# A recurrent layer and an attention layer on one core: first norm rows by products with ones, a fourth place for loaded weights, another order at several seams

## The chip, the cores and the metric

The kernel runs as one program on 1 core of a Trainium2 chip. The metric is the device time of one execution in microseconds (us); of several runs the median counts. The engines are TensorE (PE in the profile, its weight loads are PEld), VectorE (DVE), ScalarE (ACT), GpSimd (POOL) and SyncE (SP), which before the change issues every transfer.

## The reference, cut to what matters

```python
def rms_norm(x, g):
    return x * rsqrt(mean(x * x, axis=-1) + 1e-6) * g

def lru_mixer(h, ...):                       # layer 0, width 1536 in 12 blocks of 128
    u = h @ w_in                             # 1024 x 1024 times 1024 x 3072
    xb, gate = u[..., :1536], u[..., 1536:]
    xc = causal_depthwise_conv(xb, conv_w, conv_b)      # 4 taps
    r = sigmoid(block_diag(xc, wa) + ba); i = sigmoid(block_diag(xc, wx) + bx)
    log_a = -8 * r * softplus(-a_param)
    bterm = sqrt(-expm1(2 * log_a)) * (i * xc)
    hs = scan(exp(log_a), bterm)             # first-order recurrence over the sequence
    return (hs * silu(gate)) @ w_out

def fox_mixer(h, w_in, b_f, w_out):          # layer 1, 16 heads of 64
    q, k, v, gate, f_logit = split(h @ w_in) # 4 * 1024 + 16 columns
    cum = cumsum(log_sigmoid(f_logit + b_f)) # one row for each head
    logits = q @ k.T / 8 + cum[q] - cum[k]   # causal
    return (softmax(logits) @ v * silu(gate)) @ w_out

x = x + lru_mixer(rms_norm(x, norm_g[0]))
x = x + fox_mixer(rms_norm(x, norm_g[1]))
out = rms_norm(x, final_g)                   # 1024 x 1024, float32
```

## The kernel before, in words

The sequence (1024) is worked on in two halves of 512; activations lie with the features on the 128 partitions. Nearly every product is a float32 one made of three passes: each operand is split into a high part and a rest (`wh`/`wl` for weights, `hh`/`hl` for activations), and the passes are high by high, high by rest and rest by high. ScalarE makes the high part (`to_hi`, lines 80 to 92), VectorE or GpSimd the rest (`to_lo`, L96). A weight block goes through three tiles: `wf` (as loaded; 3 places), `wh` and `wl` (4 places each).

The order of instructions on each engine is set ahead of time by the language's scheduler, which follows the order of the code, generators that the code advances by hand (`run`, `take`, `drain`) and `issue_after` marks, which put an instruction behind a named one in that order. Every engine then runs its own list in order and waits on semaphores.

The program has these stages.

1. **First norm** (0 to about 58 us). The first layer's input product doesn't wait for the norm: it runs on `x * g`, and the row of inverse roots, `rs`, is multiplied in when a result is taken out of PSUM (`us`, L271, and `gps`). `inv_rms` (L136 on) makes `rs` for one half: eight products 128x1 with a column of ones sum the squares into `sscol`; ScalarE takes roots of the 128x4 result, VectorE the reciprocals (L147) and four diagonal matrices (L149); one product of ones with them spreads the row over all partitions (`rsrow`, L151), and ScalarE copies it to `rs` (L152). For n = 2 the product `ups` needs the PSUM banks that `us` of n = 0 has to empty first.
2. **Recurrent layer** (to about 430 us): a loop over 12 blocks with `ups` and `gps` products, gates, `recur` (tanh, exp, square, root, scan) and output products `ops`.
3. **Second norm, values, forget gates** (to about 510 us). `values(g)` makes V for four heads: eight sequence tiles `st`, each 8 by 3 products into one PSUM tile `vps`, which ScalarE and VectorE empty. Call 0 also makes the 16 forget logits (`fz`); `forget` transposes them (`fps`, L58), and accumulates them into `cum`, which goes through DRAM into operands `T` and `U` of the score product.
4. **Attention** (to about 1098 us): for 16 heads, `maxima` makes scores `S`, adds the mask and takes maxima `m` (L678), and exponentials `p` with row sums (L683); `weigh` transposes `p` (`pt`), splits it and multiplies by V (`O`). Beside them PE is filled with the next pair's key, query and gate products, with `values(1)` to `values(3)` after heads 3, 7 and 11, and late with output products `ops`. The inverse row sums go to DRAM and come back spread over 64 partitions (`recd`, L697, and `recb`, L701); GpSimd multiplies them into the gate (`sg`, L710) and the gate into the head's output (`yo`, L765). `split_y` splits `yo` for the last pairs (`yhh`, `yhl`). `partial` adds `ops` to `xp` and stores it to DRAM (`x1d`, L842).
5. **Turning and the last norm** (to the end). `turned` adds the last two pairs' product to the transposed residual in `turn`; ScalarE squares and sums (`sq`, L891), VectorE multiplies by the final weights, `root_mean` (L909 to L912) gives the factor, and L897/L898 scale.

Of the kernel before, what the change touches and what calls it, by code (L numbers as in the profile page):

```python
# [38 lines left out]
def trunk(ctx: ExitStack, tc: tile.TileContext, xt, w0, wg, wo0, pc, gn, gf, w1, wv, wf, bf, wo1, out):  # L39
# [57 lines left out]

    def split_weights(src, shape, hi_eng, lo_eng, parts=wpool):
        wt = wpool.tile([P, *shape], F32, tag="wf", name="wf", bufs=3)
# [75 lines left out]
    with ExitStack() as l0:  # L175
# [3 lines left out]
        tmp = lru.enter_context(pool("t0", 1, side="right"))  # L179

# [77 lines left out]

        for _ in zip(split_x(0), square_x(0)):
            pass  # L260
# [7 lines left out]
        def conv(n, ups):  # L268
# [10 lines left out]
            wt = wpool.tile([P, 4, P], F32, tag="wf", name="wgf", bufs=3)[:, :2]  # L279
# [30 lines left out]
        def recur(n, parts=(slice(0, SEQ),)):  # L310
# [4 lines left out]
            for cs in parts:  # L315
# [10 lines left out]
                nc.scalar.activation(t_, t_, AF.Sqrt, scale=1.0 / 16.0)  # L326
# [15 lines left out]
        def out_weights(g, d0):  # L342

            wt = wpool.tile([P, 4, P], F32, tag="wf", name="wf", bufs=3)
# [25 lines left out]
        for n in range(NB):  # L370
# [8 lines left out]
            if n == 0:  # L379
# [4 lines left out]
                done = rms_row(sums[0], rs[:, :HALF])[1]  # L384
# [34 lines left out]
        outputs(NB - 1, halves, silu(state[NB - 1], gps, halves))  # L419
        lru.close()  # L420
# [50 lines left out]
    with ExitStack() as l1:  # L471
# [4 lines left out]
        mask = tu.tile([P, SEQ], BF16, name="mask")  # L476
        nc.gpsimd.memset(mask, 0.0)
        nc.gpsimd.affine_select(
            out=mask, in_=mask, pattern=[[-1, SEQ]], compare_op=ALU.is_ge, fill=NEG, base=SEQ - P, channel_multiplier=1
        )  # L480


# [5 lines left out]
        for s in range(2):  # L488
            nc.gpsimd.memset(f32(T[s][64:, 1]), 1.0)
            for u in U[s][s:]:  # L490
                nc.vector.memset(f32(u[64:, 1]), 0.0)
                nc.vector.memset(f32(u[64:68, 1]), -1.0)
# [9 lines left out]
        def values(g):  # L502
# [11 lines left out]
            for st in range(8):  # L514
                if ex and st % 2:
                    pt = ps.tile([P, SEQ], F32, tag="S", name="vps")[:, : 256 + ex]
                else:
                    pt = ps.tile([P, 256 + ex], F32, tag="g", name="vps")
                c = (st % 4) * P
                for k in range(KT):  # L520
                    xh, xl = hT[st // 4][k]
                    wh, wl = parts[k]
                    xh, xl = xh[:, c : c + P], xl[:, c : c + P]
# [3 lines left out]
                    if k % 4 == 1:  # L527
                        yield
# [542 lines left out]
```

## Time and profile before

| | |
|---|---|
| three runs | 1137.04, 1137.51, 1138.75 us; median 1137.51 us |
| the profiled execution | 1138.24 us; its span, from first to last instruction, 1136.5 us |
| granted clock of TensorE | 0.999 |
| busy: VectorE, ScalarE, GpSimd | 757.9 us (67%), 592.1 us (52%), 163.5 us (14%) |
| transfers | 105.43 MB, all but the instruction queues on one hardware queue; its packets took 31.8% of the 16 engines' span |
| the chain that ended last, in its last stretches | `turn` products 18.55 us from 1112.07 us, then squares, root, reciprocal, scaling and the output's transfers to 1136.5 us |

A row of the trace's timeline reads: start, duration, engine, line, operation, result<-operands, shape, and in brackets how long the engine had been idle before it and what it had waited for. Matmuls are pipelined, so the duration of one is longer than the distance to the next; the distance between two starts is what a product costs. A row of the waits reads: total us, how many times, the longest.

### The profile page before, as it was taken

Reading aid. Unit: us, or ns where it says so; the run is one execution under the profiler, and the core shown is the slowest. Engines: PE = TensorE matmul, PEld = TensorE weight load, DVE = VectorE, ACT = ScalarE, POOL = GpSimd, SP = SyncE. Lnnn points to the kernel's source line nnn. Section 1 sums busy time; section 2 is a strip of 40 time slices with the busy share of each in tenths; the row PEclk is TensorE's granted clock in tenths of the full one; section 3 lists DMA queues with packets and bytes.
Section 4 is the critical chain, followed back from the end, with each engine's and each line's share of the span. In section 5 each row is a group of like instructions: output and inputs, shape, how many; then the busy total and the mean of one; then the engine's idle time right before and its main releaser. Section 6 shows DMA issues by size and latency. Waiting matters only on the chain.

```text
span 1136.5 us, 15822 instructions
## 1 busy us (share of the span) xinstructions
PE 1116.5 (98%) x5713; PEld 937.5 (82%) x5713; DVE 757.9 (67%) x1276; ACT 592.1 (52%) x1081; POOL 163.5 (14%) x105
## 2 busy tenths in 40 slices
PE   8999999999999999999999999999999999999997
PEld 7787888888888887888888888888888888878886
DVE  7589756876568689666676466764666645676645
ACT  8388345354453666365555355553555534554435
POOL 1212112121121201420010100101001010010110
PEclk9999999999999999999999999999999999999999
DMA  6111121111202114433525215242142431665445
GB/s 215 52 42 51 42 61 38 52 51 42 61 28 61 51 53 147 130 108 95 121 71 117 71 59 123 80 108 79 58 116 78 114 86 47 180 176 164 155 145 185
DMA packets 63702, 105.43 MB, mean 93 GB/s; under 512 B 9508, under 2 KB 24484, under 8 KB 63624
## 3 DMA queue, kind: packets, MB, share of 16 engines
q1 hardware_dynamic: 63624, 104.42, 31.8%
q8 instruction: 45, 0.74, 0.3%
q14 instruction: 33, 0.27, 0.1%
HBM read 63.30 MB, written 15.93 MB: 70 GB/s over the span
## 4 chain that ended last, share of the span: by engine, by line
PE 89%; DVE 3%; ACT 2%; issue 2%; DMA 2%; POOL 1%; SPq 0%; POOLq 0%; ACTq 0%; DVEq 0%
PE gps L54 33%; PE ops L54 15%; PE ups L54 11%; PE vps L54 7%; PE S L54 6%; PE O L54 6%; PE pt L58 5%; PE turn L54 3%; PE gate L54 2%; DVE sq L162 1%; POOL wl L96 1%; DMA x<-in_xt 1%; DVE wl L96 0%; DVE x L453 0%; DMA wf<-in_wo 0%
## 5 line engine op out<-in xcount | busy, mean ns | idle before, releaser
L54 PE MATMUL gps<-hh,wh 128*128 128x512 f32 x576 | 228.9, 398 | 0.0
L54 PE MATMUL gps<-hl,wh 128*128 128x512 f32 x576 | 226.7, 394 | 0.0
L54 PE MATMUL gps<-hh,wl 128*128 128x512 f32 x576 | 226.6, 393 | 0.0
L85 ACT CAST wh<-wf 128x512 fp32r<-128x512 f32 (+2 forms) x156 | 94.3, 607 | 144.2 <-PE gps L54 47.2
L683 ACT ACTIVATE p<-S,m 128x128 f32<-128x128 f32 (+7 forms) x128 | 94.9, 741 | 135.5 <-DVE m L678 134.4
L96 POOL TENSOR_TENSOR wl<-wf,wh 128x512 fp32r<-128x512 f32 (+1 forms) x60 | 98.1, 1639 | 395.9 <-ACT wh L85 342.8
L96 DVE TENSOR_TENSOR pl<-pt,ph 128x512 fp32r<-128x512 f32 (+1 forms) x198 | 98.6, 540 | 81.3 <-ACT ph L85 81.0
L54 PEld LDWEIGHTS gps<-hl,wh 128*128 128x128 f32 x576 | 108.2, 188 | 24.5
L54 PEld LDWEIGHTS gps<-hh,wl 128*128 128x128 f32 x576 | 108.6, 189 | 19.8
L54 PEld LDWEIGHTS gps<-hh,wh 128*128 128x128 f32 x576 | 108.5, 188 | 19.8
L678 DVE CUSTOM_DVE_ANT_0 S<-S,mask 128x128 f32<-128x128 f32 (+7 forms) x128 | 97.3, 760 | 30.5 <-PE S L54 28.9
L710 POOL TENSOR_TENSOR sg<-sg,recb 64x1024 f32<-64x1024 f32 (+1 forms) x17 | 39.2, 2306 | 460.2 <-DMA recb<-recd 444.6
L85 ACT CAST ph<-pt 128x512 fp32r<-128x512 f32 (+1 forms) x198 | 83.6, 473 | 30.6 <-PE pt L58 25.3
L54 PE MATMUL S<-T,U 96*128 96x512 f32 (+7 forms) x384 | 92.2, 349 | 2.0 <-ACT p L683 2.0
L96 DVE TENSOR_TENSOR wl<-wf,wh 128x512 fp32r<-128x512 f32 x96 | 72.1, 756 | 26.0 <-ACT wh L85 25.3
L361 DVE TENSOR_TENSOR x<-x,ops 128x512 f32<-128x512 f32 x80 | 54.0, 681 | 50.6 <-PE ops L54 50.6
L54 PEld LDWEIGHTS S<-T,U 128*128 128x128 f32 (+1 forms) x384 | 68.7, 190 | 15.9 <-ACT p L683 3.2
L54 PE MATMUL ups<-hh,wh 128*128 128x512 f32 x192 | 75.9, 395 | 4.3 <-ACT hh L87 2.4
L58 PE MATMUL pt<-ident,p 128*128 128x128 f32 x576 | 79.3, 273 | 0.0
L58 PEld LDWEIGHTS pt<-ident,p 128*128 128x128 f32 x576 | 67.4, 140 | 12.4 <-issue 2.2
L54 PE MATMUL vps<-wh,hh 128*128 128x256 f32 (+1 forms) x256 | 73.7, 288 | 3.0 <-DVE sg L649 2.1
L54 PE MATMUL ops<-yh,wh 128*128 128x512 f32 x192 | 76.1, 396 | 0.5 <-DVE x L453 0.5
(176 smaller groups left out, 2259.0 us busy)
## 6 DMA issues: line engine op xcount, KB each, us to landing
wf<-in_w SPq DMA_DIRECT2D x100, 256.0 KB
wf<-in_wo SPq DMA_DIRECT2D x64, 128.0 KB
U<-qkh SPq DMA_DIRECT2D x64, 128.0 KB
T<-qkh SPq DMA_DIRECT2D x28, 256.0 KB
x<-in_xt SPq DMA_DIRECT2D x16, 256.0 KB
x1d<-x SPq DMA_DIRECT2D x16, 256.0 KB
wf<-in_wv SPq DMA_DIRECT2D x16, 256.0 KB
U<-qkl SPq DMA_DIRECT2D x32, 128.0 KB
```

What stands on the lines that cost most here:

```text
L54: pe[0] = nc.tensor.matmul(*args, **kw)
L58: pe[0] = nc.tensor.transpose(*args)
L85: nc.scalar.copy(hi, src)
L96: return eng.tensor_tensor(lo, src, f32(hi), ALU.subtract)
L162: eng.tensor_tensor(parts[0], parts[0], sq, ALU.add)
L361: nc.vector.tensor_tensor(x, x, pt, ALU.add)
L678: nc.vector.tensor_tensor_reduce(S[:, :n], S[:, :n], mask[:, SEQ - n :], -1.0, -NEG, ALU.add, ALU.min, accum_out=m)
L683: seen[0] = nc.scalar.activation(p, S[:, :n], AF.Exp, bias=m, scale=-1.0, accum_out=sums[:, i : i + 1])
L710: nc.gpsimd.tensor_tensor(sg, sg, recs[hd // 2][rows, cs], ALU.mult)
```

## The change

Eight things are changed together.

- `norm_row` takes the place of `inv_rms` for the first norm: two float32 products 128x512 of ones with the sums of squares give the row on all partitions at once; ScalarE's root and VectorE's reciprocal then work on 128x512. The chain of small operations `softplus` stays marked to follow the first half's.
- Every fourth loaded weight block of the recurrent layer lies in a place of its own (`wx`), and the gate weights too (`wgf`), so that they no longer share the three of `wf`.
- In `recur` the root is marked to follow the gates' last tanh on ScalarE.
- `forget` yields ahead of its second half's last transposes and marks each transpose to follow the last product; what calls it spreads it between key and query products. The memsets of `T`, `U` and the mask come behind the first steps of `values(0)`.
- `values(1)` to `values(3)` first go over four of the eight parts of the contraction for the first two sequence tiles, then the other four for both; every odd tile lies in the score banks (tag `S`).
- `split_y` of pair 6 is marked to follow the last exponential.
- The transfers `recd`, `recb` and the store of `x1d` are issued by GpSimd instead of SyncE. There are 17 `recd`, 17 `recb` (the last head in two parts) and 16 stores of `x1d`.
- The last output block is made in pieces of 512, 256 and 256 columns instead of two of 512.

```diff
+        def norm_row(h):
+            row = ps.tile([P, HALF], F32, tag="O", name="rsrow")
+            for i, sq_ in enumerate(sums[h]):
+                matmul(row, onesf, sq_, start=i == 0, stop=i == len(sums[h]) - 1)
+            r_ = rs[:, halves[h]]
+            nc.scalar.activation(r_, row, AF.Sqrt, bias=epst, scale=1.0 / SEQ)
+            return nc.vector.reciprocal(r_, r_)
...
-                done = rms_row(sums[0], rs[:, :HALF])[1]
+                done = norm_row(0)
...
-                rms_row(sums[1], rs[:, HALF:])
+                norm_row(1)
...
+    def loaded(shape):
+        if spare and next(loads) % 4 == 3:
+            return spare[0].tile([P, *shape], F32, tag="wx", name="wf")
+        return wpool.tile([P, *shape], F32, tag="wf", name="wf", bufs=3)
...
-                nc.scalar.activation(t_, t_, AF.Sqrt, scale=1.0 / 16.0)
+                with tc.issue_after(s["last"].ins):
+                    nc.scalar.activation(t_, t_, AF.Sqrt, scale=1.0 / 16.0)
...
             for i in range(4):
-                transpose(pt[:HEADS, i * P : (i + 1) * P], fz[:, half * 4 + i], ident)
+                if half and i > 1:
+                    yield
+                with tc.issue_after(pe[0].ins):
+                    transpose(pt[:HEADS, i * P : (i + 1) * P], fz[:, half * 4 + i], ident)
...
-            for st in range(8):
-                if ex and st % 2:
...
+            todo = [(st, k) for st in range(8) for k in range(KT)]
+            if not ex:
+                todo[: 2 * KT] = [(st, k) for h in range(2) for st in range(2) for k in range(h * 4, h * 4 + 4)]
...
-                nc.sync.dma_start(recd[hd, b0:b1], rc[:nb])
+                nc.gpsimd.dma_start(recd[hd, b0:b1], rc[:nb])
...
-                nc.sync.dma_start(
+                nc.gpsimd.dma_start(
                     recs[pair][rows, b0 * P : b1 * P],
...
-                nc.sync.dma_start(x1d[c, :, db], x)
+                nc.gpsimd.dma_start(x1d[c, :, db], x)
...
+                parts = ((0, 4), (4, 2), (6, 2)) if c * q * b else ((0, 4), (4, 4))
...
             if hd == 14:
-                split_y(1, 6, yos[6, 1])
+                with tc.issue_after(seen[0].ins):
+                    split_y(1, 6, yos[6, 1])
...
             if hd == 13:
-                split_y(0, 6, yos[6, 0])
+                with tc.issue_after(seen[0].ins):
+                    split_y(0, 6, yos[6, 0])
```

**PE in the first norm, before.** The list runs from the last products of n = 1's first half over the second half's sums (`sscol_381`, eight rows of which the first two stand here) to the point where the second row is spread and n = 2 begins. `m2` and `ti` hold the sums of squares; 30 products of `ups_452` (n = 1) lie where the dots are.

```order
L54 MATMUL ups_451<-hh_183,wl_448 128x512
L54 MATMUL ups_451<-hl_184,wh_447 128x512
L54 MATMUL rsrow_330<-rs_168,onesf_74 128x512
L54 MATMUL sscol_381<-onesf_74,m2_201 128x1
L54 MATMUL sscol_381<-onesf_74,ti_203 128x1
...
L54 MATMUL ups_452<-hh_199,wl_448 128x512
L54 MATMUL ups_452<-hl_200,wh_447 128x512
L54 MATMUL rsrow_397<-rs_168,onesf_74 128x512
L54 MATMUL ups_567<-hh_169,wh_557 128x512
```

The same place after the change; n = 1 is `ups_423` and `ups_424`, n = 2 is `ups_539`.

```order
L54 MATMUL rsrow_314<-ti_203,onesf_74 128x512
L54 MATMUL ups_234<-hl_200,wh_144 128x512
L54 MATMUL gps_259<-hl_200,wh_151 128x512
L54 MATMUL ups_423<-hh_169,wh_413 128x512
L54 MATMUL ups_424<-hh_185,wh_413 128x512
L54 MATMUL rsrow_367<-m2_201,onesf_74 128x512
L54 MATMUL rsrow_367<-ti_203,onesf_74 128x512
L54 MATMUL ups_423<-hh_169,wl_414 128x512
...
L54 MATMUL ups_539<-hh_169,wh_529 128x512
```

The second half's row moved from the end of n = 1 to behind its first two products; 46 products of n = 1 now stand between it and n = 2's first, and all `sscol` products are gone.

**PE at `values(1)`, before.** `vps_5503` is sequence tile 0, `vps_5534` tile 1; `wh_5499` and `wl_5500` are the last weight block.

```order
L54 MATMUL O_5344<-ph_5465,v7_4012 128x128
L54 MATMUL O_5344<-pl_5466,v7_4012 128x128
L54 MATMUL vps_5503<-wh_5499,hh_3313 128x256
L54 MATMUL vps_5503<-wh_5499,hl_3314 128x256
L54 MATMUL vps_5503<-wl_5500,hh_3313 128x256
L54 MATMUL vps_5503<-wh_5499,hh_3315 128x256
L54 MATMUL vps_5503<-wh_5499,hl_3316 128x256
L54 MATMUL vps_5503<-wl_5500,hh_3315 128x256
L54 MATMUL vps_5534<-wh_5326,hh_3301 128x256
```

After the change; `vps_5475` is tile 0, `vps_5488` tile 1, `vps_5568` tile 3, `vps_5537` tile 2, and the last weight block is `wh_5471`, `wl_5472`.

```order
L54 MATMUL O_5316<-pl_5438,v7_3984 128x128
L54 MATMUL vps_5488<-wl_5466,hh_3281 128x256
L54 MATMUL vps_5488<-wh_5465,hh_3283 128x256
L54 MATMUL vps_5488<-wh_5465,hl_3284 128x256
L54 MATMUL vps_5488<-wl_5466,hh_3283 128x256
L54 MATMUL vps_5568<-wh_5298,hh_3273 128x256
...
L54 MATMUL vps_5475<-wh_5471,hh_3285 128x256
...
L54 MATMUL vps_5475<-wl_5472,hh_3285 128x256
...
L54 MATMUL vps_5537<-wh_5298,hh_3273 128x256
```

Between the head's last `O` and the first use of the last weight block stood nothing; now 8 products stand there (and 14 more ahead of `O`'s last), 15 of them ahead of the first `wl_5472`, and 23 ahead of tile 2, whose banks (tag `g`) the gate has to leave.

**ScalarE at head 13's end, before, and after the change** (two fences; `yhh` is the split of pair 6's output, `p` with 384 or 512 columns the next head's exponentials).

```order
L85 CAST wh_9538<-wf_9536 128x512
L85 CAST wh_9544<-wf_9542 128x256
L85 CAST yhh_9636<-yo_8855 128x512
L683 ACTIVATE p_9532,sums_9426<-S_9527,m_9530 128x384
L85 CAST ph_9565<-pt_9557 128x512
```

```order
L85 CAST wh_9516<-wf_9514 128x256
L720 ACTIVATE p_9504,sums_9398<-S_9499,m_9502 128x384
L85 CAST ph_9537<-pt_9529 128x512
L85 CAST ph_9540<-pt_9529 128x384
L85 CAST wh_9643<-wf_9641 128x512
L720 ACTIVATE p_9554,sums_9398<-S_9549,m_9552 128x512
L85 CAST yhh_9608<-yo_8827 128x512
```

The split moved behind two exponentials. On GpSimd's list the late part now reads as follows (before, it held only the `sg` and `yo` rows there):

```order
L734 DMA recd_3558<-rc_9797 8x128
L738 DMA recb_9800<-recd_3558 64x1024
L879 DMA x1d_93<-xp_9849 128x512
L747 TENSOR_TENSOR sg1_9106<-sg1_9106,recb_9800 64x1024
L879 DMA x1d_93<-xp_9929 128x512
```

More of the change, by code (lines that the diff above doesn't have):

```diff
@@ L96, in to_lo @@
         return eng.tensor_tensor(lo, src, f32(hi), ALU.subtract)
+    loads, spare = itertools.count(), []
+    def loaded(shape):
+        if spare and next(loads) % 4 == 3:
+            return spare[0].tile([P, *shape], F32, tag="wx", name="wf")
+        return wpool.tile([P, *shape], F32, tag="wf", name="wf", bufs=3)
     def split_weights(src, shape, hi_eng, lo_eng, parts=wpool):
-        wt = wpool.tile([P, *shape], F32, tag="wf", name="wf", bufs=3)
+        wt = loaded(shape)
         for part, sl in src:
@@ L278, in conv @@
             to_lo(xl, xc, xh, nc.vector)
-            wt = wpool.tile([P, 4, P], F32, tag="wf", name="wgf", bufs=3)[:, :2]
+            wt = tmp.tile([P, 2, P], F32, tag="wgf", name="wgf")
             nc.sync.dma_start(wt, wg[n])
@@ L342, in out_weights @@
         def out_weights(g, d0):
-            wt = wpool.tile([P, 4, P], F32, tag="wf", name="wf", bufs=3)
+            wt = loaded([4, P])
             for j in range(2):
@@ L487, in trunk, with fixed_rows @@
         U = [(U0, tu.tile([P, 2, HALF], F32R, tag=f"U{s}", name=f"U{s}")) for s in range(2)]
[L488 to L492, printed above, removed]
+        def fixed_rows():
+            for s in range(2):
+                nc.gpsimd.memset(f32(T[s][64:, 1]), 1.0)
+                for u in U[s][s:]:
+                    nc.vector.memset(f32(u[64:, 1]), 0.0)
+                    nc.vector.memset(f32(u[64:68, 1]), -1.0)
         def project(w, use, hs=(0, 1)):
@@ L631, in trunk @@
         first = values(0)
-        for _ in range(10):
-            next(first)
-        forget(0)
+        next(first)
+        next(first)
+        fixed_rows()
+        mask = tu.tile([P, SEQ], BF16, name="mask")
+        nc.gpsimd.memset(mask, 0.0)
+        nc.gpsimd.affine_select(
+            out=mask, in_=mask, pattern=[[-1, SEQ]], compare_op=ALU.is_ge, fill=NEG, base=SEQ - P, channel_multiplier=1
+        )
+        take(first, 8)
+        drain(forget(0))
         drain(first)
-        forget(1)
         gw = [None]
@@ L841, in partial @@
                 nc.vector.tensor_tensor(x, x, pt, ALU.add)
-                nc.sync.dma_start(x1d[c, :, db], x)
-        ssq = [const.tile([P, 8], F32, name=f"ssq{c}") for c in range(2)]
+                nc.gpsimd.dma_start(x1d[c, :, db], x)
+        ssq = [const.tile([P, 8 + c], F32, name=f"ssq{c}") for c in range(2)]
         left, first_half = {}, []
@@ L931, in late @@
                 late_w.append((wh, wl))
-        drain(kq_units(0, ((1, (1,)), (0, (1,)))))
+        fill = kq_units(0, ((1, (1,)), (0, (1,))))
+        gates1 = forget(1)
+        for _ in range(2):
+            next(gates1)
+            take(fill, 2)
+        drain(gates1)
+        drain(fill)
         fill = g_units(0)
@@ L1009, in finish @@
                 yield
-        run("." * 18, fill=chain(turned(1, 0), turned(1, 1)), side=finish())
+        run("." * 20, fill=chain(turned(1, 0), turned(1, 1)), side=finish())
 def layout(inputs):
```

67 lines of the change are left out of this document (38 added, 29 removed).

## The prediction

> **What bounds the kernel now.** The page comes first: who is busy, and who carries the chain that ended last.
>
> ```profile
> span 1136.5 us, 15822 instructions
> PE 1116.5 (98%) x5713; PEld 937.5 (82%) x5713; DVE 757.9 (67%) x1276; ACT 592.1 (52%) x1081; POOL 163.5 (14%) x105
> PE 89%; DVE 3%; ACT 2%; issue 2%; DMA 2%; POOL 1%; SPq 0%; POOLq 0%; ACTq 0%; DVEq 0%
> ```
>
> TensorE is busy for 98% of the span, so only two things can move the time: fewer or cheaper products, and the 20.0 us (1136.5 - 1116.5) in which it stands still. Work that goes on other engines counts for nothing unless TensorE waits for it. So the second view is the list of TensorE's waits; these are the lines that the change touches.
>
> ```profile
> PE vps L54 <- DVE sg L649: 2.1, 3, 0.7
> PE S L54 <- ACT p L683: 2.0, 2, 1.2
> PE ups L54 <- DVE us L271: 1.9, 1, 1.9
> PE fps L58 <- DVE fz L537: 1.4, 1, 1.4
> ...
> PE vps L54 <- ACT wh L85: 0.9, 3, 0.3
> ...
> PE vps L54 <- DVE wl L96: 0.7, 3, 0.2
> ...
> PE ups L54 <- POOL wl L96: 0.2, 1, 0.2
> ```
>
> They add up to 9.2 us. A wait costs a little more than its row, since the products around it are pipelined: I take the distance between two starts, less the usual distance, as the price. The third view is therefore TensorE's timeline at each of these places.
>
> **First norm rows.**
>
> ```profile
> 30.43 0.28 PE L54 MATMUL sscol<-onesf,ti 128*128 128x1 f32 x2
> 31.91 0.47 PE L54 MATMUL ups<-hl,wh 128*128 128x512 f32 x1
> 37.98 1.02 PE L54 MATMUL rsrow<-rs,onesf 128*128 128x512 f32 x2
> 38.83 0.28 PE L54 MATMUL sscol<-onesf,m 128*128 128x1 f32 x2
> 40.54 0.48 PE L54 MATMUL ups<-hh,wh 128*128 128x512 f32 x1
> 45.90 0.39 PE L54 MATMUL ups<-hl,wh 128*128 128x512 f32 x1
> 46.13 1.02 PE L54 MATMUL rsrow<-rs,onesf 128*128 128x512 f32 x2
> 49.08 0.50 PE L54 MATMUL ups<-hh,wh 128*128 128x512 f32 x1 [1.93 <-DVE us L271]
> ```
>
> The small products take 31.91 - 30.43 = 1.48 us and 40.54 - 38.83 = 1.71 us, one spreading product 38.83 - 37.98 = 0.85 us: before, 1.48 + 1.71 + 2 x 0.85 = 4.89 us. After, two products of the spreading kind for each half: 4 x 0.85 = 3.4 us. That is -1.5 us of TensorE work. Then the wait: 49.08 - 46.13 - 0.85 = 2.1 us, in which n = 2 waits until `us` has emptied its banks. After the change the second row stands behind two products of n = 1, and 46 products separate it from n = 2. One costs 46.13 - 45.90 = 0.23 us, so TensorE gets there 46 x 0.23 = 10.6 us after the row's end. In that time ScalarE's root, VectorE's two reciprocals (the first half's may still be running) and `us` must be done. What the trace doesn't show is a reciprocal of 128x512. The nearest rows, by shape:
>
> ```profile
> L692 DVE RECIPROCAL sums<-sums 128x8 f32<-128x8 f32 x15 | 3.0, 203 | 0.5
> L912 DVE RECIPROCAL ssq<-ssq 128x1 f32<-128x1 f32 x4 | 0.6, 152 | 0.0
> ```
>
> Seven more columns cost 51 ns, 7.3 ns each; 512 would cost about 3.9 us (an estimate from these rows, far outside them; the lower end is an ordinary VectorE pass over 512 columns, 0.69 us in the `sg` row further on). I take 3.9: two reciprocals 7.8, root 0.6 (the `sq` row of the tail), `us` 1.2 (twice a 512 pass less its start), together 9.6 of 10.6 us even if none overlaps; really the first reciprocal starts about 2 us ahead of the second row's end. So the wait goes, with 1 to 3 us to spare. The gates of n = 0 come 38 more products later, which covers their convolution; `softplus`, pushed behind the reciprocals, is used later still. **Place one: -3.6 us** (ends: -3.8, and -1.5 if the wait stays).
>
> **Values.** The first of three equal places:
>
> ```profile
> 638.06 0.28 PE L54 MATMUL O<-pl,v 128*128 128x128 f32 x1
> 638.64 0.39 PE L54 MATMUL vps<-wh,hh 128*128 128x256 f32 x1 [0.30 <-ACT wh L85]
> 638.86 0.28 PE L54 MATMUL vps<-wh,hl 128*128 128x256 f32 x1
> 639.37 0.39 PE L54 MATMUL vps<-wl,hh 128*128 128x256 f32 x1 [0.22 <-DVE wl L96]
> 639.71 0.28 PE L54 MATMUL vps<-wh,hl 128*128 128x256 f32 x1
> 639.83 0.28 PE L54 MATMUL vps<-wl,hh 128*128 128x256 f32 x1
> 640.81 0.39 PE L54 MATMUL vps<-wh,hh 128*128 128x256 f32 x1 [0.70 <-DVE sg L649]
> 640.07 0.69 DVE L649 SCALAR_TENSOR_TENSOR sg<-sg,gps 128x512 f32<-128x512 f32 x1
> ```
>
> A product here costs 639.83 - 639.71 = 0.12 us, the short `O` some 0.08. The three waits cost 0.58 - 0.08 = 0.50, 0.51 - 0.12 = 0.39 and 0.98 - 0.12 = 0.86 us, 1.75 together, and each leaves the next start late by 0.1 (0.22 instead of 0.12). After the change 22 products of tiles 1 and 3 come ahead of the last weight block, 7 more ahead of its rest, 8 more ahead of tile 2: the last block is needed 22 x 0.12 = 2.6 us later, tile 2 some 23 x 0.12 = 2.8 us behind `O` and 14 x 0.12 = 1.7 us later by what moved ahead of `O`. `sg` ends at 640.76, tile 2 would start at about 642.6. All three waits are covered by 1.8 us or more. What is late next: the odd tiles now lie in the score banks, so the following `S` and `pt` wait for tiles 5 and 7 to be emptied, at most one 0.37 us ScalarE pass and one 0.35 us VectorE pass, mostly beside the last products; I charge 0.1 us. **Three calls: 3 x (1.75 + 0.2 - 0.1) = -5.5 us** (ends: -6.0, and -2.5 if the new bank waits cost 1 us a call).
>
> **Forget gates.**
>
> ```profile
> 491.99 0.48 PE L54 MATMUL gps<-hh,wh 128*128 128x512 f32 x1
> 493.91 0.28 PE L58 MATMUL fps<-ident,fz 128*16 128x128 f32 x1 [1.44 <-DVE fz L537]
> 493.64 0.21 DVE L537 TENSOR_SCALAR fz<-vps,rms 128x16 f32<-128x16 f32 x1
> ```
>
> The wait costs 1.92 - 0.23 = 1.7 us. `fz` ends at 493.85; with eleven more key products ahead of it (11 x 0.23 = 2.5 us after 492.2) the transpose is reached at 494.7. The key products moved ahead need GpSimd's part of their weights, which it finishes only just then: **-1.5 us** (ends -1.7 and -0.7). The first half's `cum` and the memsets move too, but no wait of TensorE's on a score operand stands in the list, so they are at nothing while that holds.
>
> **The late scores, and the transfers on GpSimd.** One of the two waits on `p`:
>
> ```profile
> 1018.91 0.40 PE L54 MATMUL O<-pl,v 128*128 128x512 f32 x1
> 1020.53 0.73 PE L54 MATMUL S<-T,U 128*128 128x512 f32 x2 [1.23 <-ACT p L683]
> 1019.29 0.62 ACT L85 CAST yhh<-yo 128x512 fp32r<-128x512 f32 x1 [2.98 <-POOL yo L765]
> 1015.16 2.94 DVE L96 TENSOR_TENSOR wl<-wf,wh 128x512 fp32r<-128x512 f32 x1 [0.53 <-ACT wh L85]
> 1015.15 2.39 POOL L710 TENSOR_TENSOR sg<-sg,recb 64x1024 f32<-64x1024 f32 x1 [39.82 <-DMA recb<-recd]
> 1011.38 0.47 SPq L701 DMA_DIRECT2D recb<-recd  x1
> L96 DVE TENSOR_TENSOR wl<-wf,wh 128x512 fp32r<-128x512 f32 x88 | 67.1, 767 | 25.8 <-ACT wh L85 25.0
> ```
>
> It costs 1.62 - 0.23 = 1.39 us. Two things stand ahead of `p`: the split `yhh`, which moves behind it (0.52 us at least), and, through the maxima, a `wl` that took 2.94 us instead of the mean 0.77 because it began with `sg` on GpSimd and lasted as long. `sg` began 3.8 us after `recb` was issued. From GpSimd's queue the pair of transfers can be later or a little earlier; any shift of 0.1 us to the later side lets `wl` go first, and the wait goes whole. A shift that puts `sg` ahead of another `wl` costs 2.2 us of VectorE again. How long GpSimd needs to issue a transfer the trace doesn't show; the nearest rows are SyncE's 0.47 us for `recb`, and, as the upper end, a whole GpSimd pass of 2.39 us. I take 1 us, nearer to the first since nothing is computed. The second wait (0.8 us by the list, the two together 2.0) has the same neighbours. **-1.4 us** (ends -2.3; +1.5 if both collisions stay and a third is met).
>
> [...]
>
> Behind these transfers on GpSimd's queue stand only `sg`, `yo` and stores; a late `yo` holds `yhh` and the last products. Each `yo` also waits for its head's last product, which ends well after `sg` in the last head, so 1 to 3 us of delay stay covered there. SyncE loses 50 issues and what queued behind their waits.
>
> **The tail.**
>
> ```profile
> 1130.71 0.60 ACT L891 ACTIVATE sq<-turn 128x512 f32<-128x512 f32 x1 [0.82 <-PE turn L54]
> 1100.47 0.41 ACT L85 CAST yhh<-yo 128x256 fp32r<-128x256 f32 x1 [0.30 <-POOL yo L765]
> ```
>
> Twelve products of 256 columns take as long as six of 512 (12 x 0.12 against 6 x 0.23). The last square is over 256 columns: 0.41 instead of 0.60. **-0.2 us** (ends -0.4, 0). The weights' fourth place can take 0.2 us, the wait `ups` on `wl`: **-0.2** (ends -0.4, 0). The roots save table loads on ScalarE, but TensorE waits for nothing there: 0.
>
> **Sum.** -3.6 - 5.5 - 1.5 - 1.4 - 0.2 - 0.2 = -12.4 us. The profiled execution took 1138.24 us: 1125.8. It stood 0.7 us above the median of the runs (1137.51), which gives 1125.1; against that I leave 0.4 us for new small waits: **1125.5 us**, 12 us or 1.1% less.
>
> **Rivals.**
>
> 1. *The gain half lost (1131.8 us).* A second wait stands close behind each one removed: key weights behind `fps`, emptied score banks behind `vps`, `sg` against `wl`. With the worse ends of values (-2.5), forget gates (-0.7) and scores (+1.5) the sum is -3.6 - 2.5 - 0.7 + 1.5 - 0.4 = -5.7, so 1131.8 from the median. For it: in six of the seven rows the releaser is VectorE or ScalarE, which have a queue of their own behind each of these places. Against it: the new order has 1.8 us of cover at the largest term.
> 2. *The reciprocal is long (1128.7 us).* At 7 us each (13.7 ns a column) two take 14 us, the root and `us` 1.8: 15.8 against 10.6 + 2, a wait of 3.2 us where 2.1 stood. The sum becomes -12.4 + 3.2 = -9.2. Against it: the two rows give 7.3 ns a column.
> 3. *Slower (1140 us or more).* GpSimd's issuing of 50 transfers holds VectorE as `sg` held `wl`: 2.94 - 0.77 = 2.2 us each. It decides from the point where 12.4 + 2.3 = 14.7 us, that is 7 of 50, reach TensorE. For it: the 16 stores all come in the attention's last part, with `wl`, `pl` and maxima dense on VectorE. Against it: 17 `sg` rows collided the same way before, and only two waits on `p` came of it.
> 4. *Nothing moves (1137.5 us).* The waits could be set by something the list does not name. Against it: each row names one releaser, and the order of the lists did change there.
>
> **How the numbers follow.** Forecast (1123 to 1128.5) 0.55, rival 1 0.24, rival 2 0.07, rival 3 0.06, rival 4 0.05, faster than the forecast 0.03. What a measurement of this kernel can tell from no change is about 0.2%, 2.3 us. Rivals 1 and 2 end faster by more than that, apart from 0.03 of rival 1: faster 0.86, same 0.08, slower 0.06. The range takes in the better ends of all terms less a little (-3.8 - 6.0 - 1.7 - 2.3 - 0.8 = -14.6, so 1122.9, and 1 us of further luck) and rival 1: 1121.9 to 1132.5.
>
> **What would show it.** Right: no `sscol` in the first norm, four `rsrow` of 0.85 us, no wait `ups` on `us`; no wait `vps` on `sg`, `wh` or `wl` at three places; `fps` without its wait; TensorE's busy time down by about 1.5 us and its idle time from 20 to about 9. Wrong: a reciprocal row of 128x512 above 6 us, new waits of `S` or `pt` on `v`, VectorE rows two or three times their mean beside transfers of GpSimd, or a longer stretch from the last product to the end.

## The result, and the profile after

The changed kernel took 1127.35 us (median of six runs, 1123.09 to 1129.44) beside 1137.8 us of the kernel before on the same chip: a ratio of 0.9907 (0.9889 to 0.9926), 10.5 us less. The forecast was 1125.5 us. Five of the six runs lie between 1127.12 and 1129.44 us and one at 1123.09; in a second series on another chip all four lie between 1123.57 and 1124.39 us (below). The one profile of each level puts most of the difference in one place in the late attention, which is the main subject here.

The profiled execution took 1129.44 us, its span 1127.7 us, at a granted clock of 0.998. First the page, the lines that answer to those of before: span, busy time by engine, and the chain that ended last.

```profile
span 1127.7 us, 15774 instructions
PE 1114.3 (99%) x5691; PEld 936.8 (83%) x5691; DVE 758.6 (67%) x1268; ACT 589.3 (52%) x1081; POOL 195.6 (17%) x155
PE 92%; DMA 2%; DVE 2%; issue 1%; ACT 1%; SPq 1%; POOL 0%; DVEq 0%; POOLq 0%; ACTq 0%
```

TensorE stands still for 13.4 us (1127.7 - 1114.3) where it was 20.0. GpSimd has 50 instructions more, the issues of the transfers; they take 28 of its 32 us more. Next the list of TensorE's waits, without the one at the start, which is unchanged.

```profile
PE S L54 <- ACT p L720: 2.7, 1, 2.7
PE ups L54 <- ACT hh L87: 1.1, 2, 0.8
...
PE gps L54 <- DVE qkl L595: 0.6, 1, 0.6
PE ops L54 <- DVE x L474: 0.5, 2, 0.3
PE pt L58 <- DVE pl L96: 0.5, 1, 0.5
PE pt L58 <- ACT p L720: 0.3, 1, 0.3
```

The rows `vps` on `sg`, `wh` and `wl`, `ups` on `us` and `fps` on `fz` are all gone. What is new: one wait of `S` on `p` that is longer than both of before together, and short ones on `qkl` and of `pt`.

**First norm.** The timeline, VectorE and TensorE.

```profile
33.20 3.35 DVE L275 RECIPROCAL rs<-rs 128x512 f32<-128x512 f32 x1 [3.01 <-ACT rs L274]
36.63 3.35 DVE L275 RECIPROCAL rs<-rs 128x512 f32<-128x512 f32 x1
40.08 1.23 DVE L289 TENSOR_TENSOR us<-ups,rs 128x1024 f32<-128x1024 f32 x1
33.21 1.02 PE L54 MATMUL rsrow<-m,onesf 128*128 128x512 f32 x2
34.06 1.02 PE L54 MATMUL rsrow<-ti,onesf 128*128 128x512 f32 x2
45.50 0.41 PE L54 MATMUL ups<-hh,wh 128*128 128x512 f32 x1
```

The second reciprocal runs right behind the first, `us` ends at 41.3, and TensorE reaches n = 2 at 45.50 without a wait: 4.2 us of cover. A reciprocal of 128x512 takes 3.35 us, 6.5 ns a column.

**Values**, the first of the three places, TensorE and VectorE.

```profile
634.62 0.27 PE L54 MATMUL O<-pl,v 128*128 128x128 f32 x1
634.73 0.33 PE L54 MATMUL vps<-wl,hh 128*128 128x256 f32 x1
634.90 0.27 PE L54 MATMUL vps<-wh,hh 128*128 128x256 f32 x1
634.22 0.69 DVE L686 SCALAR_TENSOR_TENSOR sg<-sg,gps 128x512 f32<-128x512 f32 x1
```

The products follow the head's last `O` at their usual distance, and `sg` is done at 634.91, ahead of all that needs its banks.

**The late scores.** Here it went wrong. TensorE at the one long wait and behind it:

```profile
1046.86 0.40 PE L54 MATMUL O<-pl,v 128*128 128x512 f32 x1
1049.94 0.74 PE L54 MATMUL S<-T,U 128*128 128x512 f32 x2 [2.69 <-ACT p L720]
1051.22 0.63 PE L54 MATMUL ops<-yhh,wh 128*128 128x512 f32 x1
1051.65 0.63 PE L54 MATMUL ops<-yhh,wl 128*128 128x512 f32 x1
```

The wait costs 3.08 - 0.23 = 2.85 us. Behind it the products stand 0.43 us apart instead of 0.23: TensorE runs at half its clock. The same place in stretches of one microsecond (stretch, its length, busy time of PE, PEld, DVE, ACT, POOL, granted clock, share of the DMA engines, GB/s):

```profile
1051.00:1052.00 1.00, 1.00 (x4) 0.84 (x3) 1.00 (x3) 0.00 (x0) 0.00 (x0) 0.60 0.66 236
1053.00:1054.00 1.00, 1.00 (x4) 0.81 (x3) 0.78 (x3) 0.41 (x2) 0.27 (x1) 0.50 0.00 0
```

Eight products lose 0.20 us each, 1.6 us, so this one place costs 4.4 us, where 0.91 us stood before. What makes `p` late is on the other engines:

```profile
1041.30 1.91 SPq L109 DMA_DIRECT2D wf<-in_wo  x3
1046.15 0.41 ACT L85 CAST wh<-wf 128x256 fp32r<-128x256 f32 x1 [3.13 <-DMA wf<-in_wo]
1046.59 2.06 DVE L96 TENSOR_TENSOR wl<-wf,wh 128x256 fp32r<-128x256 f32 x1 [1.94 <-ACT wh L85]
1046.00 2.36 POOL L747 TENSOR_TENSOR sg<-sg,recb 64x1024 f32<-64x1024 f32 x1 [1.69 <-DMA recb<-recd]
1041.00 0.54 POOL L738 DMA_DIRECT2D recb<-recd  x1 [2.50 <-DMA recd<-rc]
```

SyncE issues the load of a block of output weights at 1041.30 (the first of three in the row), and ScalarE stands 3.13 us before it can split the block, 4.85 us after that issue. VectorE waits behind it for the block's rest, `wl`, with the maxima queued behind; and when `wl` could begin, `sg` had run on GpSimd since 1046.00, so that `wl` took 2.06 us (0.41 us where nothing runs beside it) and ended 0.29 us behind `sg`. The inverse row sums for `sg` come by `recb`, 256 KB, issued 0.30 us ahead of the weights' 128 KB.

**The tail** (ScalarE):

```profile
1121.46 0.38 ACT L931 ACTIVATE sq<-turn 128x256 f32<-128x256 f32 x1 [0.46 <-PE turn L54]
1123.02 0.72 ACT L941 ACTIVATE res<-res,ssq 128x512 f32<-128x512 f32 x1 [0.23 <-DVE ssq L956]
```

From the last product's start to the last scaling it is 1.93 us, before 2.08. But from there to the end of the span it is 4.66 us, before 4.17.

### The profile page after: what moved, and what is told of

Same layout as the page of the kernel before. It is cut to its first block, busy times and chain, and to the rows that moved or that the text cites. A ratio compares the mean times of both kernels' runs of the same rounds, so it can differ in the third digit from the quotient of the medians.

```text
span 1127.7 us, 15774 instructions
## 1 busy us (share of the span) xinstructions
PE 1114.3 (99%) x5691; PEld 936.8 (83%) x5691; DVE 758.6 (67%) x1268; ACT 589.3 (52%) x1081; POOL 195.6 (17%) x155
## 4 chain that ended last, share of the span: by engine, by line
PE 92%; DMA 2%; DVE 2%; issue 1%; ACT 1%; SPq 1%; POOL 0%; DVEq 0%; POOLq 0%; ACTq 0%
PE gps L54 33%; PE ops L54 16%; PE ups L54 12%; PE vps L54 8%; PE S L54 6%; PE O L54 6%; PE pt L58 5%; PE gate L54 3%; PE turn L54 3%; DMA wf<-in_wo 1%; DMA x<-in_xt 1%; POOL wl L96 0%; PE rsrow L54 0%; DMA wf<-in_w 0%; DMA yhl<-y1d 0%
## 5 line engine op out<-in xcount | busy, mean ns | idle before, releaser
L96 POOL TENSOR_TENSOR wl<-wf,wh 128x512 fp32r<-128x512 f32 (+1 forms) x60 | 101.0, 1689 | 389.8 <-ACT wh L85 362.5
L54 PE MATMUL ups<-hl,wh 128*128 128x512 f32 x192 | 76.7, 399 | 0.2
L54 PE MATMUL ups<-hh,wl 128*128 128x512 f32 x192 | 76.2, 397 | 0.0
```

The costliest lines, as they stand in the source:

```text
L54: pe[0] = nc.tensor.matmul(*args, **kw)
L96: return eng.tensor_tensor(lo, src, f32(hi), ALU.subtract)
```

## The experiments

The theory after the first result: the late place costs 4.4 us because a late load of weights and GpSimd's `sg` meet there, and GpSimd's queue has a part in it only by when `sg` starts. The rivals: the transfers on GpSimd are themselves the cause, by what their issue takes from VectorE; the load is late alone, whatever runs beside it; or the parts do less than the traces say. Intervals are of the ratio to the kernel before, whose median was 1137.95, 1137.99 and 1138.34 us in the three series.

### The late place

**The changed kernel again**, unedited, on another chip.

> The changed kernel once more, as the base of this set. Both theories: median 1126 to 1128 us with a spread of 3 us or more. If the spread comes from the scores' wait near 1047 us (sg on GpSimd beginning together with a late wl on VectorE), then a profile near 1129 us shows that wait with 2 to 3 us and a halved clock behind it, and a profile near 1123 us shows neither.

1123.78 us, ratio 0.9874 (0.9858 to 0.9891). The expected spread of 3 us didn't come: the four runs lie within 0.8 us. What was expected of a profile near 1123 us did: its list has no wait of `S`. The place:

```profile
1040.06 1.90 SPq L109 DMA_DIRECT2D wf<-in_wo  x3
1041.17 0.54 POOL L738 DMA_DIRECT2D recb<-recd  x1 [3.96 <-DMA recd<-rc]
1042.47 0.41 ACT L85 CAST wh<-wf 128x256 fp32r<-128x256 f32 x1 [0.69 <-DMA wf<-in_wo]
1043.32 0.41 DVE L96 TENSOR_TENSOR wl<-wf,wh 128x256 fp32r<-128x256 f32 x1
1045.56 2.39 POOL L747 TENSOR_TENSOR sg<-sg,recb 64x1024 f32<-64x1024 f32 x1 [2.47 <-DMA recb<-recd]
```

The same program, the same order; but GpSimd waited 3.96 instead of 2.50 us for `recd`, so `recb` was issued 1.1 us *behind* the load. The block could be split 2.41 us after its load's issue, and `wl` was done 1.8 us before `sg` began. So the place has two outcomes. Idle time is 9.6 us here (span 1121.9, busy 1112.3), and the span is 5.8 us shorter than in the first profile.

**The three transfers back on SyncE**, all else as changed.

```diff
-                nc.gpsimd.dma_start(recd[hd, b0:b1], rc[:nb])
+                nc.sync.dma_start(recd[hd, b0:b1], rc[:nb])
...
-                nc.gpsimd.dma_start(x1d[c, :, db], x)
+                nc.sync.dma_start(x1d[c, :, db], x)
```

> The changed kernel with recd, recb and the stores of x1d issued by SyncE again. Theory A (the issue on GpSimd is what made the late scores' wait 2.7 us instead of 0.8): the wait goes back to 0.9 us or less, the clock stays whole, 1123 to 1124.5 us. Theory B (the wait comes from sg meeting a late wl, whoever issues the transfers): the wait stays between 0.8 and 2.7 us, 1125 to 1128 us. Theory C (the transfers on GpSimd are worth something of their own, since SyncE's list is freed): 1128 us or more.

1124.56 us, ratio 0.988 (0.9865 to 0.9895): as the changed kernel on the same chip. By the size of the wait (0.4 us in the list) this is what Theory A expected, but the changed kernel itself had no such wait on this chip, so the run doesn't decide between the theories. The collision is there all the same, smaller:

```profile
1044.23 2.39 POOL L747 TENSOR_TENSOR sg<-sg,recb 64x1024 f32<-64x1024 f32 x1 [24.48 <-DMA recb<-recd]
1045.60 1.30 DVE L96 TENSOR_TENSOR wl<-wf,wh 128x256 fp32r<-128x256 f32 x1 [0.43 <-ACT wh L85]
```

**`sg` in pieces of 256 columns**, so that one instruction of GpSimd is short.

```diff
-            nc.gpsimd.tensor_tensor(sg, sg, recs[hd // 2][rows, cs], ALU.mult)
+            for o in range(0, cs.stop - cs.start, 256):
+                nc.gpsimd.tensor_tensor(sg[:, o : o + 256], sg[:, o : o + 256], rb[:, o : o + 256], ALU.mult)
```

> The changed kernel with sg multiplied in pieces of 256 columns instead of 1024. If an operation of VectorE with two operands in SBUF is held for the whole of the GpSimd operation that began before it, wl near 1047 us is held for 0.7 us at most (1.0 to 1.1 us instead of 2.06), the scores' wait falls from 2.7 to about 1.7 us without a halved clock, 1124 to 1125.5 us. If the two only share a bandwidth, wl stays at about 2 us and the time at 1126 to 1128 us.

1124.62 us, ratio 0.9881 (0.9867 to 0.9896).

```profile
1044.39 2.98 POOL L749 TENSOR_TENSOR sg<-sg,recb 64x256 f32<-64x256 f32 x4 [1.53 <-DMA recb<-recd]
1044.94 0.46 DVE L96 TENSOR_TENSOR wl<-wf,wh 128x256 fp32r<-128x256 f32 x1 [1.76 <-ACT wh L85]
```

`wl` could begin 0.2 us before the first of the four pieces ended, and took 0.46 us, not the 2 us expected if the two engines only shared a bandwidth: it was held to the end of one piece, as beside a whole `sg`, behind which it ended by 0.28 to 0.29 us (before, in the first profile after, and with the transfers on SyncE). The trace of before has more of such rows. Seven `wl` of 512 columns that began while a product of GpSimd ran took 1.35 to 2.94 us and ended 0.55 us behind it; three that began ahead of one took 0.68, as they do alone (0.69). The 15 `x` rows of that size beside one, which read PSUM, took 0.65 to 0.69 us, alone 0.68. That it takes two operands in SBUF, as the expectation has it, isn't shown: three casts `wgh`, with one operand, took 0.88 to 1.19 us beside one, 0.29 alone. Over the whole run the `wl` rows beside an `sg` take about 1.3 us above their median, in the first profile 7.2. A wait of `S` of 0.8 us is left; that is the late load's own part.

**The loads of `late` (the last pairs' output weights) in a place of their own** (the room of `xp`), so that the block in question needn't wait behind them for one of the three of `wf`.

```diff
-                    wt = wpool.tile([P, 4, P], F32, tag="wf", name="wf", bufs=3)
+                    wt = at.tile([P, 4, P], F32, tag="xp", name="wf", bufs=2)
```

> The changed kernel with the last weights (woh, wol) loaded through two places of their own instead of the three that they share with the output weights wf. Theory B: wl is no longer late there, it is done before sg begins, the scores' wait near 1047 us goes, the clock stays whole, 1122.5 to 1124 us with a small spread. Theory A: sg meets another operation of VectorE instead, 1126 to 1128 us.

1124.55 us, ratio 0.9878 (0.9863 to 0.9892), 0.5 us above the range expected; no wait of `S`, as expected. `wl` is done 6.6 us before `sg`:

```profile
1038.28 0.40 DVE L96 TENSOR_TENSOR wl<-wf,wh 128x256 fp32r<-128x256 f32 x1
1045.33 2.39 POOL L747 TENSOR_TENSOR sg<-sg,recb 64x1024 f32<-64x1024 f32 x1 [3.91 <-DMA recb<-recd]
```

These three don't differ in time from the changed kernel of the same series, which had drawn the good outcome there. They show the mechanism, not a gain.

### One part alone, on the kernel before

**`values` in the new order and tiles, nothing else.**

```diff
-            for st in range(8):
...
+            todo = [(st, k) for st in range(8) for k in range(KT)]
+            if not ex:
+                todo[: 2 * KT] = [(st, k) for h in range(2) for st in range(2) for k in range(h * 4, h * 4 + 4)]
```

> The kernel before with the change to values(1) to values(3) alone. The forecast's theory: its three places lose their waits, 5.5 us less (ratio 0.9952), the rest of the trace as before. Rival (gain given back by emptied score banks, 1 us a call): 2.5 us less (0.9978).

1132.85 us, ratio 0.9957 (0.9945 to 0.9968): -5.1 us.

**`norm_row` for the first norm, nothing else.**

```diff
-                done = rms_row(sums[0], rs[:, :HALF])[1]
+                done = norm_row(0)
```

> The kernel before with the first norm's rows by products with ones alone. The forecast's theory: no small products and no wait on us, 3.6 us less (ratio 0.9968). Rival (the reciprocals are late for n = 2): 0 to 1.5 us less.

1133.48 us, ratio 0.996 (0.9946 to 0.9973): -4.5 us.

**The three transfers on GpSimd, nothing else.**

```diff
-                nc.sync.dma_start(recd[hd, b0:b1], rc[:nb])
+                nc.gpsimd.dma_start(recd[hd, b0:b1], rc[:nb])
...
-                nc.sync.dma_start(x1d[c, :, db], x)
+                nc.gpsimd.dma_start(x1d[c, :, db], x)
```

> The kernel before with recd, recb and the stores of x1d issued by GpSimd and nothing else changed. Theory B (only the moment at which sg meets wl moves): 1.5 us less to 2 us more, by the late scores' waits alone (1.4 and 0.9 us in the trace before). Theory A (the issue on GpSimd itself holds VectorE): 2 us or more slower, with long VectorE rows beside the transfers.

1141.23 us, ratio 1.0034 (1.0021 to 1.0048): alone they make the kernel slower, by 3.2 us. That is more than the 2 us that Theory B allowed; the long VectorE rows beside the transfers, which Theory A expected, aren't there (see rival 3 below).

**The forget gates spread among key products.** The edit takes in the moved memsets and one thing that the list of changes doesn't name: the second half's first key and query results are taken out of PSUM by ScalarE, no longer by VectorE.

```diff
-                eng = nc.vector if pair == 0 else nc.scalar
...
+                    eng = nc.scalar if pair or h else nc.vector
...
+                if half and i > 1:
+                    yield
+                with tc.issue_after(pe[0].ins):
+                    transpose(pt[:HEADS, i * P : (i + 1) * P], fz[:, half * 4 + i], ident)
```

> The kernel before with the change to forget, to the memsets and to the first key and query products alone. The forecast's theory: the wait of fps goes (1.5 us), nothing else, ratio 0.9987. Rival: the moved memsets are also what took away the wait of vps on GpSimd's wl near 470 us (0.9 us), and a new wait on qkl near 504 us takes 0.6 to 0.75 us back: 1.7 to 1.9 us less (0.9984).

1138.07 us in ten runs, ratio 1.0001 (0.9991 to 1.001): no gain, within 1 us. The wait of `fps` is gone, but soon after it a product waits for `qkl`, which stands on VectorE behind the second half's accumulation (`cum`) and its parts (`cp`). The changed kernel shows the same:

```profile
501.37 1.27 DVE L648 TENSOR_TENSOR_SCAN cum<-unit,cum,z 16x512 f32<-16x512 f32 x1
504.69 0.67 DVE L595 SCALAR_TENSOR_TENSOR qkl<-gps,qkh 128x512 fp32r<-128x512 f32 x1
505.41 0.50 PE L54 MATMUL gps<-hh,wh 128*128 128x512 f32 x1 [0.59 <-DVE qkl L595]
```

### Which transfer costs, and the sum of the mends

**Only `recd` and `recb` on GpSimd**, on the kernel before.

```diff
-                nc.sync.dma_start(recd[hd, b0:b1], rc[:nb])
+                nc.gpsimd.dma_start(recd[hd, b0:b1], rc[:nb])
...
-                nc.sync.dma_start(
+                nc.gpsimd.dma_start(
                     recs[pair][rows, b0 * P : b1 * P],
```

> The kernel before with recd and recb alone on GpSimd. If the 3.4 us that the three transfers cost on the kernel before lie in when sg meets wl, then here: 1 to 3 us slower, with the late scores' waits at 2 us or more; 0.5 us of it at the end. If they lie in the stores of x1d, 0.5 us slower.

1142.31 us, ratio 1.0036 (1.0024 to 1.0048): 4.0 us slower, the whole loss, and more than the 1 to 3 us expected. At the second late place of the kernel before:

```profile
1059.29 2.36 POOL L710 TENSOR_TENSOR sg<-sg,recb 64x1024 f32<-64x1024 f32 x1 [3.98 <-DMA recb<-recd]
1059.86 2.07 DVE L96 TENSOR_TENSOR wl<-wf,wh 128x256 fp32r<-128x256 f32 x1 [1.24 <-ACT wh L85]
1063.22 0.73 PE L54 MATMUL S<-T,U 128*128 128x512 f32 x2 [2.62 <-ACT p L683]
```

and a microsecond of its clock behind that wait, in the columns given above:

```profile
1065.00:1066.00 1.00, 1.00 (x3) 0.72 (x3) 0.88 (x3) 0.09 (x1) 0.00 (x0) 0.50 0.17 56
```

The wait at the first late place (1.39 us at 1018.91 before) is gone here, with no mark on `split_y`. But the edit moved more than the transfers: on ScalarE's list `p` now stands ahead of `yhh`, where before `yhh` stood ahead, and so it is in all three kernels that got transfers on GpSimd alone. At the second place, TensorE waits 2.79 instead of 0.91 us, and half clock (0.50) follows. (Together, by the profile: 1.9 us of wait and 1.6 of half clock at the second place, 1.4 less at the first, 0.2 at the end, and 1.6 more of half clock behind the first norm's wait, which this edit doesn't touch; the last section has that wait in six profiles.) The profiles, put side by side, tell why the second place got worse. The columns: `recb`'s issue against the issue of the block's load (minus: ahead of it), the time from that load's issue to ScalarE's split, the start of `sg` ahead of that split, and what TensorE's wait costs.

| profile | `recb` against load | load to split | `sg` ahead | wait of `S` |
|---|---|---|---|---|
| before (`recb` on SyncE) | -1.20 | 3.41 | 0.72 | 0.91 |
| before, `x1d` on GpSimd | -1.21 | 3.52 | 0.91 | 0.85 |
| changed, transfers on SyncE | -1.34 | 3.13 | 0.93 | 0.6 |
| before, three on GpSimd | -0.26 | 4.36 | 0.11 | 2.45 |
| before, `recd` and `recb` on GpSimd | -0.21 | 4.45 | 0.13 | 2.79 |
| changed, first profile | -0.30 | 4.85 | 0.15 | 2.85 |
| changed, `sg` in pieces | -0.26 | 4.66 | 0.11 | 0.95 |
| changed, second profile | +1.11 | 2.41 | -3.09 | none |

With SyncE `recb` stands 1.2 us or more ahead of the load. From GpSimd it is issued just ahead of it, both transfers are under way at once, the split can begin about 1.2 us later, and it and `sg` come within 0.15 us of one another: `wl` meets nearly the whole of `sg`. The packets of the two transfers show it. Before, those of `recb` ran from 1054.15 to 1055.79 us and the load's 128 from 1056.11 to 1056.98, one after the other; with `recd` and `recb` on GpSimd they ran from 1056.21 to 1058.33 and from 1056.52 to 1058.66, side by side. The three other profiles with `recb` on SyncE at this place (`values`, first norm or forget gates alone) fit the table: -1.20 to -1.37 and 3.20 to 3.49. Only where `recd` was slow, and `recb` fell behind the load, did the weights win. That changes the theory in one point: the load was not late of itself, the transfer moved to GpSimd made it so. What sets the time that `recd` takes (2.50 or 3.96 us of waiting for it) isn't shown.

**Only the store of `x1d` on GpSimd**, on the kernel before.

```diff
-                nc.sync.dma_start(x1d[c, :, db], x)
+                nc.gpsimd.dma_start(x1d[c, :, db], x)
```

> The kernel before with the stores of x1d alone on GpSimd. If the 3.4 us lie in recd and recb: 0.5 us slower, at the end. If they lie in the stores, which stand ahead of sg in GpSimd's list and wait for the sums: 2 to 3 us slower, with sg late and the waits on p longer.

1137.81 us in ten runs, ratio 0.9994 (0.9984 to 1.0003): no difference, where 0.5 us more or 2 to 3 had been expected.

**The changed kernel with the last weights' own place and `sg` in pieces.**

```diff
-                    wt = wpool.tile([P, 4, P], F32, tag="wf", name="wf", bufs=3)
+                    wt = at.tile([P, 4, P], F32, tag="xp", name="wf", bufs=2)
...
+            for o in range(0, cs.stop - cs.start, 256):
```

> The changed kernel with the last weights in places of their own and sg in pieces, transfers still issued by GpSimd. Against the run with all three edits this leaves the issue on GpSimd alone: 0.4 to 0.9 us more at the end and nothing in the attention (Theory B), 1123 to 1124.5 us; 2 us or more if the issue itself holds an engine (Theory A).

1123.7 us, ratio 0.9871 (0.9854 to 0.9887).

**The same, and the three transfers on SyncE.**

```diff
-                nc.gpsimd.dma_start(recd[hd, b0:b1], rc[:nb])
+                nc.sync.dma_start(recd[hd, b0:b1], rc[:nb])
...
-                nc.gpsimd.dma_start(x1d[c, :, db], x)
+                nc.sync.dma_start(x1d[c, :, db], x)
```

> The changed kernel with three edits together: the transfers issued by SyncE again, the last weights loaded through places of their own, sg in pieces of 256 columns. Theory B: no wait on p is left, since wl comes early and can't be held for long; the stretch from the last scaling to the end falls from 4.6 to 4.2 us; 1122.5 to 1123.5 us. Rival: the three don't add, another wait comes up in the attention, 1124 to 1126 us.

1123.29 us, ratio 0.9872 (0.9857 to 0.9887). Neither has a wait of `S`, and their eight runs lie between 1122.65 and 1125.22. Both equal the better outcome of the changed kernel, within the ranges expected; from the last scaling to the end it is 5.09 us in the first and 4.17 in the second. In their profiles the block is split 7 us or more ahead of `sg`; that this keeps the worse outcome away for good is likely from the mechanism, and not shown, since on their chip the changed kernel wasn't run.

## Why the prediction was right, and where it was not

| term | predicted | first profile after | second profile after | alone, by time |
|---|---|---|---|---|
| first norm | -3.6 | -3.6 | -3.6 | -4.5 |
| values | -5.5 | -6.1 | -6.1 | -5.1 |
| forget gates | -1.5 | -1.6 + 0.75 | wait gone, `qkl` 0.5 in the list | 0.0 |
| late scores, transfers | -1.4 | -1.4 + 3.5 | -2.3 | +3.2 (transfers alone) |
| tail | -0.2 | -0.15 + 0.5 | end also 4.63 us | |
| fourth place for weights | -0.2 | -0.4 | -0.4 | |
| not predicted | | -0.9 + 1.1 | -0.9 | |
| span | -12.4 | -8.8 | -14.6 | |

1. *First norm: right.* All steps came as told, with 4.2 us of cover instead of 1 to 3, in part because the reciprocal took 3.35 and not the estimated 3.9 us. Rival 2, the long reciprocal, is out. Alone it gave 4.5 us, more than its rows; the last section gives a likely reason.
2. *Values: right, a little too small.* The three waits (5.2 us) and the late restarts went, and the 0.1 us a call for emptied score banks isn't in the trace. Rival 1 took this term at its worse end, -2.5; it did not come to that.
3. *Forget gates: the step "at nothing" failed.* The wait went as predicted, but "the first half's `cum` and the memsets ... are at nothing" looked only at score operands. Close behind stands a wait of another kind: `qkl` empties a PSUM bank that a later product needs, and it comes after the second half's `cum` and `cp` on VectorE's list, which did not get earlier by as much as TensorE did. By the changed kernel's trace half of the term is left; the run with this part alone shows no gain, within 1 us. In its profile 0.8 us of the 1.7 come back at `qkl`, and 0.5 in longer waits of `S` (1.67 and 1.16 us against 1.39 and 0.91); whether these belong to the part is open.
4. *Late scores: the step that failed is "any shift of 0.1 us to the later side lets `wl` go first, and the wait goes whole".* It fails at both places. At the first, `wl` going first isn't enough. With the first norm alone changed it began 0.53 us ahead of `sg` and took its usual 0.69 us, and the wait of `S` still cost 1.70 us, because `p` stands on ScalarE behind `yhh`, and `yhh` waits for `yo`, which follows `sg` on GpSimd:

```profile
1009.06 0.69 DVE L96 TENSOR_TENSOR wl<-wf,wh 128x512 fp32r<-128x512 f32 x1 [0.51 <-ACT wh L85]
1009.59 2.41 POOL L719 TENSOR_TENSOR sg<-sg,recb 64x1024 f32<-64x1024 f32 x1 [39.93 <-DMA recb<-recd]
1013.46 0.62 ACT L85 CAST yhh<-yo 128x512 fp32r<-128x512 f32 x1 [3.28 <-POOL yo L774]
1013.98 0.57 ACT L692 ACTIVATE p<-S,m 128x384 f32<-128x384 f32 x1
1014.70 0.74 PE L54 MATMUL S<-T,U 128*128 128x512 f32 x2 [1.53 <-ACT p L692]
```

   With the forget gates alone it is the same (1.67 us). With `recd` and `recb` alone on GpSimd `wl` also went first, and `p` ran ahead of `yhh`; there the wait is gone:

```profile
1019.09 0.58 ACT L683 ACTIVATE p<-S,m 128x384 f32<-128x384 f32 x1 [0.85 <-DVE m L678]
1021.56 0.62 ACT L85 CAST yhh<-yo 128x512 fp32r<-128x512 f32 x1 [1.79 <-POOL yo L765]
```

   And with the stores of `x1d` alone on GpSimd `p` ran ahead of `yhh` but `wl` was held for 2.86 us, and 0.77 us of wait were left. The prediction had named both causes; by these runs the move of `yhh` alone takes 0.6 us off the 1.39, `wl` first alone takes nothing off, and only the two together take the whole. The changed kernel has both: its mark puts `yhh` behind `p`, and `wl` went first. At the second place the step moved `sg` and held `wl`'s time fixed, and there the two hang together: `recb` from GpSimd's queue travels beside the load that `wl` needs, makes that load later, and meets it. So the term is +2.1 us in the first profile, beyond its worse end of +1.5, and its better end, -2.3, in the second. A second cost wasn't in the sum at all: half clock behind the wait, 1.6 us. That the time came within 1.9 us of the forecast in spite of this is in part luck: values gave 0.6 us more than predicted, and a wait of 0.9 us went that nobody had counted.
5. *Rival 3 (GpSimd's issuing holds VectorE): shown false as a mechanism, near in effect.* An issue takes 0.52 to 0.70 us of GpSimd in the first profile after (0.56 in the median), and over 80 VectorE rows that lie beside one take no longer than others unless an `sg` is there too; 16 stores of `x1d` alone cost nothing. (The prediction's argument against this rival, that 17 `sg` rows collided before, counts too many: in the profile before, 7 `wl` rows lie beside an `sg` and 3 of them were held.) Yet the transfers alone make the kernel before 0.34% slower, through what `recb` meets. From its issue to `sg` it is 3.9 us with SyncE (1052.88 to 1056.77) and 4.5 us with GpSimd (1054.76 to 1059.29). The first packet of `recb` came 1.27 us behind its issue by SyncE and 1.45 by GpSimd, in the same two profiles. The prediction's step that any shift to the later side lets `wl` win held at the first late place and failed at the second. What an `sg` can do to VectorE stands in the `wl` rows: 2.94 us (512 columns) and 2.06 and 2.07 us (256) beside a whole `sg`, 0.46 us beside pieces, 0.69 and 0.41 alone.
6. *Tail: right in its step, -0.15 us, and taken back behind it.* With GpSimd issuing transfers, last scaling to end takes 4.23 to 5.10 us in eight profiles, with SyncE alone 4.16 to 4.18 in six. Which part of the end grows isn't shown.

The first profile's balance (-3.6 - 6.1 - 1.6 + 0.75 - 1.4 + 3.5 - 0.15 + 0.5 - 0.4 - 0.9 + 1.1 = -8.3) comes within 0.5 us of the 8.8. The -0.4 is the wait of `ups` on `wl` near 106 us that the fourth place was to take; the -0.9 is a wait of `vps` on a `wl` of GpSimd's near 470 us, and the +1.1 are two small ones of `pt`. Both waits on `wl` are also missing from some profiles of the kernel before with another part changed, the one near 470 us with the first norm alone, the one near 106 us with `values` alone, so they can't be put down to the change for certain. Without the second late place the balance would be -11.8, next to the forecast. That the four runs from 1127.12 to 1128.2 us had the same wait as the profiled one at 1129.44 is inferred from the size (4.4 us against the 3.7 us between the two levels), and whether half clock followed in each of them is open.

Parts alone don't add up: -5.1 - 4.5 + 0.1 + 3.2 = -6.3 us, the whole is -14.2 us in its second series. The transfers' +3.2 falls away where `wl` comes early. The other 4.7 us must lie in what was not tried alone (the place of `yhh`, the fourth place for weights, the tail) or in how the parts meet; no run separates these.

## What to carry to other kernels

An instruction that is held until another engine's ends, as `wl` was beside `sg` (2.06 us instead of 0.41), can turn a shift of a microsecond into a wait nearly two longer (2.79 us instead of 0.91): where a part moves the start of one, price it by the starts of *both*, and ask whether the transfer that moves one also travels beside the load that the other waits for; make that load early, or the long instruction short, rather than hope that the order falls well. A wait of TensorE can be dearer than its row: behind five of the nine waits of 2.0 to 2.85 us here the granted clock fell to 0.50 for about 3.4 us, which cost about 1.6 us more. A wait that is removed shows what stands next on the releaser's own queue; read that queue before you book the gain. And an edit that only changes which engine issues a transfer can reorder another engine's list, as `p` and `yhh` changed places here: compare the lists of all engines before a part is called alone.

## What the runs showed of the hardware that was not expected

- *The clock halves behind short waits.* Over the 14 profiles and past the first 20 us there are nine waits of TensorE of 2.0 us or more. Behind 2.85 and 2.79 us the granted clock fell to 0.50 for 3.4 us (from 1051.20 to 1054.61 us in the first profile after; eight products at 0.43 instead of 0.23 us, 1.6 us lost), behind 2.45 us it did not, and behind the first norm's wait of 2.1 us, the same in six profiles of kernels that still have it, it fell in three:

```profile
49.00:50.00 1.00, 1.00 (x3) 0.75 (x3) 0.88 (x1) 1.00 (x1) 1.00 (x1) 0.52 0.08 25
50.00:51.00 1.00, 1.00 (x4) 0.75 (x3) 0.95 (x1) 0.98 (x2) 0.13 (x1) 0.50 0.00 0
```

  These are rows of the kernel with `values` alone; before shows 1.00 in both stretches. Behind waits of 1.7 us or less no fall was seen. The length alone doesn't tell which of the nine are followed by one: this wait is 1.9 us in the lists of both kernels. With `values` alone the product behind it began at 48.80 us, and from the 0.52 of the stretch above the clock fell at 49.04; before, it began at 49.08 us, and the clock stayed at 1.00. That its place in time decides is the author's inference from these nine waits, and isn't shown. So the first norm's wait cost 2.1 us, or 3.7 where half clock followed, and taking it away can be worth more than its row.
- *A reciprocal on VectorE* costs 6.5 ns a column at 128x512 (3.35 us), next to the 7.3 that the rows of 1 and 8 columns had given.
- *The end of a program whose GpSimd issues transfers* is up to 0.9 us longer from the last scaling on (5.10 against 4.17 us), long after the last of these transfers.
